# A hybrid decoder layer's expert phase: gates put into the one-hots by ScalarE, expert numbers found by row and column, the second product opened with the first tiles, and the second table's rows spread over all its tiles

## The chip, the core and the metric

The kernel runs on one core of one Trainium2 chip. The metric is device time in microseconds (us) of one execution. A kernel's time is the median of its runs. Times inside an execution come from one profiled execution, which has a time of its own.

## The reference, cut to what matters

The layer is a residual block: a mixer (RWKV-7 and dilated attention) gives `h`, and then 8 heads of a product-key expert layer add to it. Only the expert part is touched here. There are 512 tokens, 16384 experts, and 8 x 16 = 128 chosen experts for each token.

```python
def peer(u, peer_wq, peer_k1, peer_k2, peer_u, peer_v):
    ...
    v1, i1 = lax.top_k(s1, PEER_TOPK)                 # 16 of 128 row keys
    v2, i2 = lax.top_k(s2, PEER_TOPK)                 # 16 of 128 column keys
    cand = (v1[..., :, None] + v2[..., None, :]).reshape(cshape)
    cidx = (i1[..., :, None] * PEER_N_KEYS + i2[..., None, :]).reshape(cshape)
    top, sel = lax.top_k(cand, PEER_TOPK)             # 16 of 256 pairs
    idx = jnp.take_along_axis(cidx, sel, axis=-1)
    gate = jax.nn.softmax(top, axis=-1)
    ...
        ue = jnp.take(peer_u, ic, axis=0)
        act = jax.nn.gelu(jnp.einsum('cd,ced->ce', uc, ue).astype(jnp.float32), approximate=False)
        ve = jnp.take(peer_v, ic, axis=0)
        return jnp.einsum('ce,ced->cd', (gc * act).astype(ve.dtype), ve)
```

## The kernel before, in words

Tokens 0 to 127 are done as the reference does it, with gathered rows: GpSimd (POOL) gathers one expert row for every token of the group (128 gathers from `u`, 128 from `v`, 524 KB each, line 1146), and VectorE (DVE) takes the dot product (line 1155) or accumulates the row times its gate (line 1169). Six row buffers (`NUG`) are shared by both tables.

Tokens 128 to 511 (384 tokens) are done densely over all experts. **Product one** goes over 128 tiles of `uT`, each 128 experts: `gemm_ch` loads the tile (`wraw`, 512 KB, queue of SyncE, SP), splits it into a high part (`whi`, ScalarE (ACT), line 127) and a low part (`wlo`, DVE, line 128), and TensorE (PE) does 24 matmuls of 384 columns, three for each of 8 blocks. There are four buffers for the split tiles. ScalarE takes the result out of one of the two `mm` banks by a gelu (line 1208), and the tile goes to DRAM (`act_d`) unless it is one of NR = 8 tiles that stay in SBUF; these are the last 8.

Beside product one run two background programs. `rows_u` is the gathers from the first table. `routing` alternates `topk` and `scatter`. `topk` finds the 16 best pairs of each token among 50 candidates (`cand`), with the pair's expert number in `cidx` (POOL adds); it gets the number out by a one-hot of 16 x 50 (`eq`, lines 1081 to 1084) for each head. `scatter` spreads the gates into a dense matrix G[expert, token], four tokens a step, 96 steps: one one-hot of the column index for four tokens (`ohE`, DVE, line 1127), four one-hots of the row index that are multiplied by the gate in the same instruction (`ohA`, DVE, line 1131), four matmuls of 128 columns in fp32 (line 1137, eight records, in the four banks `c` to `f` by turns), and an ACT copy into `Gs` (line 1138). Every 8 steps ACT writes a 2 MB block to DRAM (`g_d`).

**Product two** goes over 128 tiles of `v`. A `G` block (8 tiles, 1.5 MB) and the gelu tile `act` are loaded by SP, DVE multiplies them (line 1249), ACT makes `wh` (line 1255) and DVE `wl` (line 1256), and 18 matmuls of 512 columns add the tile's part to six banks (`mm`, `mm`, `a`, `a`, `c`, `d`), which stay open over all 128 tiles. The order of the tiles begins with the eight kept ones (120 to 127). `G` holds gates of every token, so it needs the last `g_d` write. `rows_v` runs beside it.

The order of instructions on each engine comes from a scheduler with a simulated timeline (`schedule_with_timeline_sim`): ready work is put earlier than the code says, so the order on the engines is not that of the loops. Each engine, and each DMA queue with it, then works strictly in its order. Two conditions hold whatever the scheduler does: the pool `vg`, with `G`, `wh` and `wl`, takes the place of `pp`, the pool of `topk` and `scatter`, so none of its tiles exists before that pool is closed; and `vp`, with the residual `hfin`, takes the place of `n2`, which the last matmul of product one reads.

Of the kernel before, what the change touches and what calls it, by code (L numbers as in the profile page):

```python
# [100 lines left out]
class Kern:  # L101
# [947 lines left out]
    def topk(self, pp, i, res):  # L1049
# [5 lines left out]
        nc.vector.tensor_scalar(xf[:, :, 0], xf[:, :, 0], 128.0, None, op0=OP.mult)  # L1055
        cand = pp.tile([P, 8, NCAND], F32, tag="cand", name="cand")
        cidx = pp.tile([P, 8, NCAND], F32, tag="cidx", name="cidx")
# [20 lines left out]
        xs = pp.tile([P, 8, 16], F32, tag="xs", name="xs")  # L1078
        for h in range(8):
            eq = pp.tile([P, 16, NCAND], F32, tag="eq", name="eq", bufs=2)  # L1080
            nc.vector.tensor_tensor(eq, self.iota[:, None, :NCAND].to_broadcast([P, 16, NCAND]),
                                    posf[:, h, :, None].to_broadcast([P, 16, NCAND]), op=OP.is_equal)
            nc.vector.tensor_tensor(eq, eq, cidx[:, h, None, :].to_broadcast([P, 16, NCAND]), op=OP.mult)
            nc.vector.tensor_reduce(xs[:, h], eq, axis=AX.X, op=OP.add)
            if h % 2:
                yield
# [8 lines left out]
        if i == 0:  # L1095
            xi = self.gp.tile([P, 8, 16], I32, name="xi0")
            nc.vector.tensor_copy(xi, xs)
# [5 lines left out]
        xi = pp.tile([P, 8, 16], I32, tag="xi", name="xi")  # L1103
        x2 = pp.tile([P, 8, 16], I32, tag="x2", name="x2")
        nc.vector.tensor_copy(xi, xs)
        nc.vector.tensor_scalar(x2, xi, 127, None, op0=OP.bitwise_and)
        nc.vector.tensor_copy(sel[:, 1], x2)
        nc.vector.tensor_scalar(x2, xi, 7, None, op0=OP.logical_shift_right)
        nc.vector.tensor_copy(sel[:, 0], x2)
# [8 lines left out]
    def scatter(self, pp, i, res):  # L1118
# [67 lines left out]
    def phase_peer(self, es):  # L1186
# [7 lines left out]
        self.iota = pp.tile([P, 128], F32, name="iota")  # L1194
# [6 lines left out]
        done = 0  # L1201
        for i1 in range(128):
            acc = self.gemm_ch(I["uT"][i1], KT, n2h, n2l)
            if i1 < 128 - NR:
# [4 lines left out]
            if i1 < 128 - NR:  # L1209
# [12 lines left out]
        order = list(range(128 - NR, 128)) + list(range(128 - NR))  # L1222
# [4 lines left out]
        rows = self.rows_v(acc0)  # L1227
        LAST = 4
# [8 lines left out]
        for n, i1 in enumerate(order):  # L1237
            if n % GI == 0:
                G = vg.tile([P, TD // GB, GI, GB], F32, tag="G", name="G", bufs=2)
# [104 lines left out]
```

## Time and profile before

| | |
|---|---|
| median of 3 runs | 2067.61 us (2065.8 to 2068.58) |
| the profiled execution: its time | 2073.24 us |
| the profiled execution: its span | 2071.4 us |
| mean granted TensorE clock | 0.975 of full speed |
| PE busy | 1959.7 us, 95% of the span |
| DVE busy | 1606.0 us, 78% |
| ACT busy | 938.4 us, 45% |
| POOL busy | 639.8 us, 31% |
| DMA | 519.45 MB, mean 251 GB/s |
| PE work on the chain that ended last | 62%; DVE 17%, DMA 11% |

The span is the time between the first and the last instruction that the profiler saw; the execution's own time is 1.84 us longer. The experts take the stretch from about 870 us to the end. The shares are means over stages with different limits, so the rows further down are taken stage by stage.

### The profile page before, as it was taken

Reading aid. Unit: us, or ns where it says so; the run is one execution under the profiler, and the core shown is the slowest. Engines: PE = TensorE matmul, PEld = TensorE weight load, DVE = VectorE, ACT = ScalarE, POOL = GpSimd, SP = SyncE. Lnnn points to the kernel's source line nnn. Section 1 sums busy time; section 2 is a strip of 40 time slices with the busy share of each in tenths; the row PEclk is TensorE's granted clock in tenths of the full one; section 3 lists DMA queues with packets and bytes.
Section 4 is the critical chain, followed back from the end, with each engine's and each line's share of the span. In section 5 each row is a group of like instructions: output and inputs, shape, how many; then the busy total and the mean of one; then the engine's idle time right before and its main releaser. Section 6 shows DMA issues by size and latency. Waiting matters only on the chain.

```text
span 2071.4 us, 34017 instructions
## 1 busy us (share of the span) xinstructions
PE 1959.7 (95%) x12529; PEld 1699.5 (82%) x12529; DVE 1606.0 (78%) x3192; ACT 938.4 (45%) x1454; POOL 639.8 (31%) x511
## 2 busy tenths in 40 slices
PE   5998899999998979999999999999959999989999
PEld 4676677788877868899999999999948887778887
DVE  7476895955645548999999999877769988888555
ACT  3756666564354343343344544466623333334332
POOL 2324650331411110005755445400034555450000
PEclk9999989999999989999999999999979999999999
DMA  6666855356556313248988999965499999998763
GB/s 267 212 205 194 254 175 148 107 194 217 175 184 213 128 62 120 92 163 315 356 332 325 363 347 349 371 250 215 172 364 365 394 397 369 397 363 322 227 214 115
DMA packets 236299, 519.45 MB, mean 251 GB/s; under 512 B 35554, under 2 KB 129506, under 8 KB 233572
## 3 DMA queue, kind: packets, MB, share of 16 engines
q1 hardware_dynamic: 180260, 334.27, 47.1%
q0 software_dynamic: 36864, 134.23, 17.3%
q10 hardware_dynamic: 19008, 48.77, 6.2%
q8 instruction: 99, 1.62, 0.3%
q14 instruction: 68, 0.56, 0.1%
HBM read 432.23 MB, written 84.97 MB: 250 GB/s over the span
## 4 chain that ended last, share of the span: by engine, by line
PE 62%; DVE 17%; DMA 11%; issue 5%; ACT 3%; POOL 2%; SPq 0%; DVEq 0%; ACTq 0%; POOLq 0%
PE ps_mm L141 14%; PE ps_mm L143 13%; PE ps_mm L142 13%; DMA act<-act_d 4%; PE gps L1137 4%; DVE wlo L128 4%; DVE row L1155 2%; DMA wada<-in_wada 2%; PE ps_a L143 2%; PE ps_a L141 2%; PE ps_a L142 2%; DMA wraw<-in_v 2%; DVE acc L1169 1%; DMA G<-g_d 1%; POOL acc L443 1%
## 5 line engine op out<-in xcount | busy, mean ns | idle before, releaser
L127 ACT ACTIVATE whi<-wraw 128x1024 fp32r<-128x1024 f32 x356 | 370.1, 1042 | 399.7 <-PE ps_mm L142 223.6
L128 DVE TENSOR_TENSOR wlo<-wraw,whi 128x1024 fp32r<-128x1024 f32 x356 | 431.9, 1216 | 133.4 <-ACT whi L127 128.3
L141 PE MATMUL ps_mm<-n2h,whi 128*128 128x384 f32 (+1 forms) x1152 | 400.3, 348 | 3.2 <-ACT act L1208 3.2
L142 PE MATMUL ps_mm<-n2l,whi 128*128 128x384 f32 (+1 forms) x1152 | 398.4, 346 | 0.0
L143 PE MATMUL ps_mm<-n2h,wlo 128*128 128x384 f32 (+1 forms) x1152 | 396.2, 345 | 2.2 <-DVE wlo L128 2.2
L1146 POOL DMA_INDIRECT row<-in_v,xi x128 | 196.9, 1538 | 346.1 <-DVE acc L1169 173.1
L1146 POOL DMA_INDIRECT row<-in_u,xi x128 | 186.9, 1460 | 171.9 <-DVE dots L1155 133.6
L141 PEld LDWEIGHTS ps_mm<-n2h,whi 128*128 128x128 f32 x1152 | 218.5, 190 | 9.1 <-ACT act L1208 4.4
L143 PEld LDWEIGHTS ps_mm<-n2h,wlo 128*128 128x128 f32 x1152 | 218.3, 190 | 8.3 <-DVE wlo L128 3.4
L142 PEld LDWEIGHTS ps_mm<-n2l,whi 128*128 128x128 f32 x1152 | 218.5, 190 | 4.7
L141 PE MATMUL ps_mm<-n1h,whi 128*128 128x512 f32 x464 | 191.9, 417 | 6.5 <-ACT n1h L271 5.0
L1255 ACT ACTIVATE wh<-act 128x384 fp32r<-128x384 f32 x128 | 66.8, 526 | 280.1 <-DVE act L1249 148.9
L142 PE MATMUL ps_mm<-n1l,whi 128*128 128x512 f32 x464 | 190.3, 410 | 0.2 <-DVE n1l L272 0.2
L143 PE MATMUL ps_mm<-n1h,wlo 128*128 128x512 f32 x464 | 190.2, 410 | 0.0
L1169 DVE SCALAR_TENSOR_TENSOR acc<-row,g,acc 128x1024 f32<-128x1024 f32 x127 | 162.3, 1278 | 0.8
L1155 DVE CUSTOM_DVE_ANT_0 row<-row,n2t 128x1024 f32<-128x1024 f32 x128 | 153.0, 1217 | 0.5 <-DMA row<-in_u,xi 0.5
L1249 DVE TENSOR_TENSOR act<-act,G 128x384 f32<-128x384 f32 x128 | 69.9, 553 | 105.3 <-DMA act<-act_d 90.6
L1138 ACT ACTIVATE Gs<-gps 128x512 f32<-128x512 f32 x96 | 107.0, 1120 | 57.1 <-PE gps L1137 55.1
L141 PE MATMUL ps_mm<-whi,wh 128*128 128x512 f32 x256 | 93.1, 397 | 33.8 <-ACT wh L1255 33.8
L141 PEld LDWEIGHTS ps_mm<-n1h,whi 128*128 128x128 f32 x464 | 90.7, 197 | 29.3 <-ACT n1h L271 5.0
L142 PEld LDWEIGHTS ps_mm<-n1l,whi 128*128 128x128 f32 x464 | 90.6, 195 | 21.2 <-issue 2.5
L143 PEld LDWEIGHTS ps_mm<-n1h,wlo 128*128 128x128 f32 x464 | 91.0, 196 | 20.7 <-issue 0.8
(406 smaller groups left out, 3883.0 us busy)
## 6 DMA issues: line engine op xcount, KB each, us to landing
wraw<-in_uT SPq DMA_DIRECT2D x128, 512.0 KB, 5.5
wraw<-in_v SPq DMA_DIRECT2D x128, 512.0 KB, 7.9
wraw<-in_win SPq DMA_DIRECT2D x60, 512.0 KB, 4.0
g_d<-Gs ACTq DMA_DIRECT2D x12, 2048.0 KB, 10.3
G<-g_d SPq DMA_DIRECT2D x16, 1536.0 KB, 11.9
act_d<-act ACTq DMA_DIRECT2D x120, 192.0 KB, 5.2
act<-act_d SPq DMA_DIRECT2D x120, 192.0 KB, 8.2
wada<-in_wada SPq DMA_DIRECT2D x64, 256.0 KB, 4.2
```

What stands on the lines that cost most here:

```text
L127: nc.scalar.activation(hi[:, :n], raw[:, :n], AF.Copy)
L128: nc.vector.tensor_tensor(lo[:, :n], raw[:, :n], hi[:, :n].bitcast(F32), op=OP.subtract)
L141: mm(acc, lh, rh, start=start, stop=False)
L142: mm(acc, lh, rl, start=False, stop=False)
L143: mm(acc, ll, rh, start=False, stop=stop)
L1137: nc.tensor.matmul(g[:, j], E[:, j], A[:, j], start=True, stop=True)
L1138: nc.scalar.activation(Gs[:, :, o:o + 4].rearrange("p i t -> p t i"), g, AF.Copy)
L1146: self.nc.gpsimd.indirect_dma_start(row, None, self.I[tab], bass.IndirectOffsetOnAxis(ap=self.xi[:, n:n + 1], axis=0))
L1155: self.gathered(self.rowp, n, "u", lambda row: nc.vector.tensor_tensor_reduce(out=row, in0=row, in1=self.n2t, scale=1.0, scalar=0.0, op0=O ...
L1169: nc.vector.scalar_tensor_tensor(acc, row, self.gates0[:, n:n + 1], acc, op0=OP.mult, op1=OP.add)
L1249: nc.vector.tensor_tensor(act.rearrange("p (b t) -> p b t", t=GB), act.rearrange("p (b t) -> p b t", t=GB), G[:, :, n % GI, :], op=OP.mult)
L1255: nc.scalar.activation(wh, act, AF.Copy)
```

## The change

In `topk`, the expert number is no longer read out of `cidx`, which is gone with its POOL adds. Row and column are found apart: `ge` says which candidate rows begin at or before the position, its product with the steps `dx` between neighbouring row keys sums up to the row, and its product with the lengths of the rows gives the position inside the row, whose one-hot picks the column. Two heads go in one instruction, so there are 16 groups of 8 instructions of 512 elements in place of 32 groups of 3 instructions of 800 elements. The second and third sums go straight into `sel`, so the casts and shifts that took a number apart are gone. The constant `iota` grows from 128 to 160 columns.

In `scatter`, one DVE instruction makes both one-hots for four tokens (`ohAE`, 1024 elements, three buffers), and ACT multiplies the four row one-hots by the gates (128 columns each, the gate as a per-partition scale).

In `phase_peer`, the kept tiles are 0 to 7, product two goes over its tiles in order 0 to 127, the background has to be done by tile 112 in place of 119, the pool `pp` is closed there and the first `G` block is asked for. Three tiles are weighed (`act` times `G`, `wh`, `wl`) while product one still runs, and the banks are filled in the order `a`, `c`/`d`, `mm`. In the code `rows_v` takes n x 128 // 118 steps by tile n in place of one for each tile and a second one at every sixteenth from 80 on.

```diff
@@ topk
-        nc.vector.tensor_scalar(xf[:, :, 0], xf[:, :, 0], 128.0, None, op0=OP.mult)
+        dx = pp.tile([P, 8, 16], F32, tag="dx", name="dx")
+        nc.vector.tensor_copy(dx[:, :, 0:1], xf[:, :, 0, 0:1])
+        nc.vector.tensor_tensor(dx[:, :, 1:], xf[:, :, 0, 1:], xf[:, :, 0, :15], op=OP.subtract)
...
-            nc.gpsimd.tensor_tensor(cidx[:, :, o:o + n], xf[:, :, 0, p:p + 1].to_broadcast([P, 8, n]),
-                                    xf[:, :, 1, 0:n], op=OP.add)
...
-        for h in range(8):
-            eq = pp.tile([P, 16, NCAND], F32, tag="eq", name="eq", bufs=2)
-            nc.vector.tensor_tensor(eq, self.iota[:, None, :NCAND].to_broadcast([P, 16, NCAND]),
-                                    posf[:, h, :, None].to_broadcast([P, 16, NCAND]), op=OP.is_equal)
-            nc.vector.tensor_tensor(eq, eq, cidx[:, h, None, :].to_broadcast([P, 16, NCAND]), op=OP.mult)
-            nc.vector.tensor_reduce(xs[:, h], eq, axis=AX.X, op=OP.add)
...
+        for h0 in range(0, 8, 2):
...
+            nc.vector.tensor_tensor(ge, ph[:, :, None].to_broadcast([P, n, 16]), row(128), op=OP.is_ge)
+            nc.vector.tensor_tensor(by_head(eq), by_head(ge), dx[:, hs, None, :].to_broadcast([P, 2, 16, 16]), op=OP.mult)
+            nc.vector.tensor_reduce(sel[:, 0, hs].rearrange("p h k -> p (h k)"), eq, axis=AX.X, op=OP.add)
+            nc.vector.tensor_tensor(ge, ge, row(144), op=OP.mult)
+            off = pp.tile([P, n], F32, tag="off", name="off", bufs=2)
+            nc.vector.tensor_reduce(off, ge, axis=AX.X, op=OP.add)
+            nc.vector.tensor_tensor(off, ph, off, op=OP.subtract)
+            nc.vector.tensor_tensor(eq, off[:, :, None].to_broadcast([P, n, 16]), row(0), op=OP.is_equal)
+            nc.vector.tensor_tensor(by_head(eq), by_head(eq), xf[:, hs, 1, None, :].to_broadcast([P, 2, 16, 16]), op=OP.mult)
+            nc.vector.tensor_reduce(sel[:, 1, hs].rearrange("p h k -> p (h k)"), eq, axis=AX.X, op=OP.add)
@@ scatter
-            nc.vector.tensor_tensor(E, self.iota[:, None, :].to_broadcast([P, 4, 128]),
-                                    sl[:, 1, t4:t4 + 4, None].to_broadcast([P, 4, 128]), op=OP.is_equal)
+            AE = pp.tile([P, 2, 4, 128], F32, tag="ohAE", name="ohAE", bufs=3)
+            A, E = AE[:, 0], AE[:, 1]
+            nc.vector.tensor_tensor(AE, self.iota[:, None, None, :128].to_broadcast([P, 2, 4, 128]),
+                                    sl[:, 0:2, t4:t4 + 4, None].to_broadcast([P, 2, 4, 128]), op=OP.is_equal)
             for j in range(4):
                 t = t4 + j
-                nc.vector.tensor_scalar(A[:, j], self.iota, sl[:, 0, t:t + 1], sl[:, 2, t:t + 1],
-                                        op0=OP.is_equal, op1=OP.mult)
+                nc.scalar.activation(A[:, j], A[:, j], AF.Copy, scale=sl[:, 2, t:t + 1])
@@ phase_peer
+        def weigh(i1, act):
+            nc.vector.tensor_tensor(act.rearrange("p (b t) -> p b t", t=GB), act.rearrange("p (b t) -> p b t", t=GB),
+                                    Gs[i1 - i1 % GI][:, :, i1 % GI, :], op=OP.mult)
...
+            nc.scalar.activation(wh, act, AF.Copy)
+            nc.vector.tensor_tensor(wl, act, wh.bitcast(F32), op=OP.subtract)
...
-            if i1 < 128 - NR:
+            if i1 >= NR:
                 act = ap.tile([P, TD], F32, tag="act", name="act", bufs=4)
...
-            while done < min(i1 + 1, 10) + max(i1 - 9, 0) * 96 // 104:
+            while done < min(i1 + 1, 10) + max(i1 - 9, 0) * 96 // 98:
...
-            if i1 == 119:
+            if i1 == 112:
                 run(bg)
                 e1.close()
                 vg = self.pool(es, "vg")
+                load_g(0)
+            elif i1 >= 120 and i1 % 2 == 0 and len(ready) < 3:
+                weigh(len(ready), keep[len(ready)])
...
-        order = list(range(128 - NR, 128)) + list(range(128 - NR))
...
-                for t in out:
+                for t in (2, 3, 1):
...
-            next(rows, None)
-            if n > 64:
-                next(rows, None) if n % 16 == 0 else None
+            while vdone < n * 128 // 118:
+                next(rows_v, None)
+                vdone += 1
```

How the instructions of SyncE's queue stand around the end of product one. Before (`wraw<-in_uT` and `wraw<-in_v` are the weight tiles of product one and two; the first row comes after ten earlier `uT` loads):

```order
L124 DMA wraw<-in_uT 128x1024 x117
L1248 DMA act<-act_d 128x384 x3
L124 DMA wraw<-in_uT 128x1024
L1248 DMA act<-act_d 128x384
L124 DMA wraw<-in_v 128x1024 x8
L1240 DMA G<-g_d 128x12x256 x2
L1242 DMA hfin<-h_d 128x4x1024
L1243 DMA gt_15109<-gt_d 128x1024
L1240 DMA G<-g_d 128x12x256
L124 DMA wraw<-in_v 128x1024 x5
```

And now, on the same queue and again after ten earlier loads:

```order
L124 DMA wraw<-in_uT 128x1024 x107
L1212 DMA G<-g_d 128x12x256 x2
L124 DMA wraw<-in_uT 128x1024 x2
L1212 DMA G<-g_d 128x12x256
L124 DMA wraw<-in_uT 128x1024 x9
L124 DMA wraw<-in_v 128x1024 x7
L1267 DMA hfin<-h_d 128x4x1024
L1273 DMA act<-act_d 128x384 x3
L1268 DMA gt_15011<-gt_d 128x1024
L124 DMA wraw<-in_v 128x1024 x2
```

The two `G` loads were behind the first eight tiles of `v`; they now stand eleven tiles of `uT` before the end of product one. The residual `hfin` and the first `act` loads stand between the tiles of `v`.

How ScalarE's instructions stand in the scatter stretch, late in product one. Before (`whi` is the high part of the next weight tile, `act` the gelu, `Gs` the copy of a scatter step):

```order
L127 ACTIVATE whi<-wraw 128x1024
L1208 ACTIVATE act<-ps_mm 128x384
L1210 DMA act_d<-act 128x384
L1138 ACTIVATE Gs<-gps 128x4x128 x2
L127 ACTIVATE whi<-wraw 128x1024
L1208 ACTIVATE act<-ps_mm 128x384
```

And now (`ohAE` is the gate's multiplication into the row one-hots, four for each step):

```order
L1137 ACTIVATE ohAE<-ohAE,sl 128x128 x8
L1232 ACTIVATE act<-ps_mm 128x384
L1143 ACTIVATE Gs<-gps 128x4x128
L1234 DMA act_d<-act 128x384
L1137 ACTIVATE ohAE<-ohAE,sl 128x128 x4
L1143 ACTIVATE Gs<-gps 128x4x128 x2
L1137 ACTIVATE ohAE<-ohAE,sl 128x128 x4
L1145 DMA g_d<-Gs 128x4096
L1137 ACTIVATE ohAE<-ohAE,sl 128x128 x4
L127 ACTIVATE whi<-wraw 128x1024
```

Every scatter step now has two visits on ScalarE, one ahead of its matmuls and one behind them. On DVE the 96 pairs of one-hots stand between the `wlo` of `uT` tile 39 and that of tile 108; before, they stood between that of tile 47 and that of `v` tile 3.

How DVE's instructions stand in product two, while rows of the second table come in. Before (`acc` takes one gathered row):

```order
L1169 SCALAR_TENSOR_TENSOR acc_15110<-row,g_8687,acc_15110 128x1024
L1249 TENSOR_TENSOR act<-act,G 128x384
L1169 SCALAR_TENSOR_TENSOR acc_15110<-row,g_8687,acc_15110 128x1024
L1256 TENSOR_TENSOR wl<-act,wh 128x384
L1249 TENSOR_TENSOR act<-act,G 128x384
L128 TENSOR_TENSOR wlo<-wraw,whi 128x1024
L1256 TENSOR_TENSOR wl<-act,wh 128x384
L1169 SCALAR_TENSOR_TENSOR acc_15110<-row,g_8687,acc_15110 128x1024 x2
L1249 TENSOR_TENSOR act<-act,G 128x384
L128 TENSOR_TENSOR wlo<-wraw,whi 128x1024
```

And now:

```order
L1174 SCALAR_TENSOR_TENSOR acc_15012<-row,g_8689,acc_15012 128x1024
L1216 TENSOR_TENSOR act<-act,G 128x384
L1174 SCALAR_TENSOR_TENSOR acc_15012<-row,g_8689,acc_15012 128x1024
L1223 TENSOR_TENSOR wl<-act,wh 128x384
L1174 SCALAR_TENSOR_TENSOR acc_15012<-row,g_8689,acc_15012 128x1024 x2
L1216 TENSOR_TENSOR act<-act,G 128x384
L128 TENSOR_TENSOR wlo<-wraw,whi 128x1024
L1223 TENSOR_TENSOR wl<-act,wh 128x384
L1216 TENSOR_TENSOR act<-act,G 128x384
L128 TENSOR_TENSOR wlo<-wraw,whi 128x1024
L1223 TENSOR_TENSOR wl<-act,wh 128x384
```

The rows are grouped otherwise, but in both orders 12 stand to every 8 tiles, and the last row stands behind the `wlo` of `v` tile 85 before and of tile 86 now.

## Rows read from the trace of the kernel before

**Rows 1.** One line's instructions: gelu of product one (ns min/median/max, first and last start us).

```profile
L1208 ACT ACTIVATE act<-ps_mm x128: 466/472/553, 873.1 to 1497.5; 128x384 f32<-128x384 f32 x128
```

**Rows 2.** Timeline of ACT: gelus nine tiles apart, and two neighbours in the scatter stretch.

```profile
1001.69 0.49 ACT L1208 ACTIVATE act<-ps_mm 128x384 f32<-128x384 f32 x1 [3.67 <-PE ps_mm L143]
...
1039.13 0.49 ACT L1208 ACTIVATE act<-ps_mm 128x384 f32<-128x384 f32 x1 [1.20 <-PE ps_mm L143]
...
1402.13 0.47 ACT L1208 ACTIVATE act<-ps_mm 128x384 f32<-128x384 f32 x1
...
1408.09 0.47 ACT L1208 ACTIVATE act<-ps_mm 128x384 f32<-128x384 f32 x1
```

**Rows 3.** Windows in product one: us, PE, PEld, DVE, ACT, POOL busy (count), PEclk, DMA share, GB/s.

```profile
1048.00:1112.00 64.00, 59.05 (x332) 57.23 (x331) 64.00 (x135) 26.91 (x34) 29.43 (x22) 0.92 0.84 305
1360.00:1480.00 120.00, 120.00 (x809) 120.00 (x808) 91.34 (x226) 74.28 (x83) 0.00 (x0) 1.00 0.57 209
```

**Rows 4.** Timeline from product one to product two: start, us, engine, line [idle before <-releaser].

```profile
1501.44 1.17 PE L1137 MATMUL gps<-ohA,ohE 128*128 128x128 f32 x8 [1.60 <-DVE ohA L1131]
...
1503.74 0.33 ACTq L1140 DMA_DIRECT2D g_d<-Gs  x1
...
1511.23 4.29 SPq L1240 DMA_DIRECT2D G<-g_d  x2
...
1523.13 3.84 DVE L1249 TENSOR_TENSOR act<-act,G 128x384 f32<-128x384 f32 x8 [14.45 <-DMA G<-g_d]
...
1524.30 0.79 PE L141 MATMUL ps_mm<-whi,wh 128*128 128x512 f32 x1 [21.69 <-ACT wh L1255]
```

**Rows 5.** Windows there: the wait itself, and two microseconds behind it (columns as before).

```profile
1503.70:1524.30 20.60, 0.00 (x0) 0.00 (x0) 6.04 (x7) 0.59 (x3) 5.82 (x5) 0.52 1.00 355
...
1526.00:1528.00 2.00, 2.00 (x6) 1.52 (x6) 2.00 (x4) 0.00 (x0) 0.00 (x0) 0.50 1.01 398
```

**Rows 6.** Timeline of PE: two tiles of product two, and the last matmul.

```profile
2030.10 0.39 PE L141 MATMUL ps_mm<-whi,wh 128*128 128x512 f32 x1
...
2034.18 0.39 PE L141 MATMUL ps_mm<-whi,wh 128*128 128x512 f32 x1
...
2065.91 0.39 PE L143 MATMUL ps_d<-whi,wl 128*128 128x512 f32 x1
```

**Rows 7.** Windows in product two: two with rows of `v` coming in, one after the last.

```profile
1524.30:1684.00 159.70, 159.70 (x696) 132.08 (x697) 146.42 (x171) 56.82 (x77) 85.31 (x55) 0.99 1.02 383
1684.00:1884.00 200.00, 188.27 (x812) 152.52 (x811) 172.42 (x199) 67.12 (x89) 97.38 (x63) 0.99 1.02 379
1924.00:2044.00 120.00, 120.00 (x531) 99.36 (x530) 67.05 (x94) 45.01 (x62) 0.00 (x0) 1.00 0.64 208
```

**Rows 8.** PE's waits from 1530 to the end: us in total, times, longest.

```profile
PE ps_mm L141 <- ACT wh L1255: 12.1, 9, 3.4
```

**Rows 9.** DMA from 1530 to 1880.

```profile
DMA packets 54262, 133.15 MB, mean 380 GB/s; under 512 B 4457, under 2 KB 29142, under 8 KB 54239
```

**Rows 10.** DVE's groups by form, 865 to 1510: xcount | busy us, mean ns | idle before.

```profile
L1131 DVE TENSOR_SCALAR ohA<-iota,sl 128x128 f32<-128x128 f32 x384 | 106.6, 342 | 0.0
L1127 DVE TENSOR_TENSOR ohE<-iota,sl 128x512 f32<-128x512 f32 x96 | 65.6, 683 | 8.9 <-PE gps L1137 8.8
L1081 DVE TENSOR_TENSOR eq<-iota,posf 128x800 f32<-128x800 f32 x32 | 30.9, 979 | 0.0
```

**Rows 11.** ACT's groups by form, whole span or from 865 to 1510.

```profile
L127 ACT ACTIVATE whi<-wraw 128x1024 fp32r<-128x1024 f32 x129 | 136.3, 1063 | 181.4 <-PE ps_mm L142 137.7 <-DMA wraw<-in_uT 22.9 <-issue 4.3
L1138 ACT ACTIVATE Gs<-gps 128x512 f32<-128x512 f32 x96 | 107.0, 1120 | 57.1 <-PE gps L1137 55.1
L441 ACT ACTIVATE wada<-wada,silc 128x512 f32<-128x512 f32 x56 | 39.5, 717 | 37.3 <-DMA wada<-in_wada 37.1
L884 ACT ACTIVATE sc<-sc,ot 128x128 f32<-128x128 f32 x32 | 12.4, 390 | 11.8 <-DVE ot L882 10.5 <-issue 1.3
```

**Rows 12.** Timeline of ACT: three instructions with a per-partition scale, back to back.

```profile
267.07 1.93 ACT L441 ACTIVATE wada<-wada,silc 128x512 f32<-128x512 f32 x3
```

More of the change, by code (lines that the diff above doesn't have):

```diff
@@ L1102, in topk @@
             return
[L1103 to L1109, printed above, removed]
         tp = self.ps("a")
@@ L1193, in phase_peer @@
         pp = self.pool(e1, "pp")
-        self.iota = pp.tile([P, 128], F32, name="iota")
+        self.iota = pp.tile([P, 160], F32, name="iota")
         nc.sync.dma_start(self.iota, I["iota"])
@@ L1201, in phase_peer, with load_g @@
         done = 0
+        ready, Gs = {}, {}
+        LAST = 4
+        def load_g(i1):
+            G = Gs[i1] = vg.tile([P, TD // GB, GI, GB], F32, tag="G", name="G", bufs=2)
+            nc.sync.dma_start(G, self.g_d[:, :, i1:i1 + GI, :].rearrange("b p i t -> p b i t"))
+        def weigh(i1, act):
+            nc.vector.tensor_tensor(act.rearrange("p (b t) -> p b t", t=GB), act.rearrange("p (b t) -> p b t", t=GB),
+                                    Gs[i1 - i1 % GI][:, :, i1 % GI, :], op=OP.mult)
+            tail = i1 >= 128 - LAST
+            bufs, tg, pool = (LAST, "f", vp) if tail else (3, "", vg)
+            wh = pool.tile([P, TD], F32R, tag="wh" + tg, name="wh", bufs=bufs)
+            wl = pool.tile([P, TD], F32R, tag="wl" + tg, name="wl", bufs=bufs)
+            nc.scalar.activation(wh, act, AF.Copy)
+            nc.vector.tensor_tensor(wl, act, wh.bitcast(F32), op=OP.subtract)
+            ready[i1] = wh, wl
         for i1 in range(128):
             acc = self.gemm_ch(I["uT"][i1], KT, n2h, n2l)
-            if i1 < 128 - NR:
+            if i1 >= NR:
                 act = ap.tile([P, TD], F32, tag="act", name="act", bufs=4)
@@ L1226, in phase_peer @@
         acc0 = vp.tile([P, D], F32, name="acc0")
-        rows = self.rows_v(acc0)
-        LAST = 4
+        rows_v = self.rows_v(acc0)
+        vdone = 0
         def mms(t, f, ws, n):
@@ L1236, in phase_peer @@
         last = []
-        for n, i1 in enumerate(order):
-            if n % GI == 0:
-                G = vg.tile([P, TD // GB, GI, GB], F32, tag="G", name="G", bufs=2)
-                nc.sync.dma_start(G, self.g_d[:, :, i1:i1 + GI, :].rearrange("b p i t -> p b i t"))
+        for n in range(128):
+            if n % GI == 0 and n not in Gs:
+                load_g(n)
             if n == 64:
@@ L1243, in phase_peer @@
                 nc.sync.dma_start(gt2, self.gt2_d)
-            if i1 in keep:
-                act = keep[i1]
-            else:
-                act = ap.tile([P, TD], F32, tag="act", name="act", bufs=4)
-                nc.sync.dma_start(act, self.act_d[i1])
-            nc.vector.tensor_tensor(act.rearrange("p (b t) -> p b t", t=GB), act.rearrange("p (b t) -> p b t", t=GB),
-                                    G[:, :, n % GI, :], op=OP.mult)
-            bufs = LAST if n >= 128 - LAST else 3
-            tg = "f" if n >= 128 - LAST else ""
-            wh = (vp if tg else vg).tile([P, TD], F32R, tag="wh" + tg, name="wh", bufs=bufs)
-            wl = (vp if tg else vg).tile([P, TD], F32R, tag="wl" + tg, name="wl", bufs=bufs)
-            nc.scalar.activation(wh, act, AF.Copy)
-            nc.vector.tensor_tensor(wl, act, wh.bitcast(F32), op=OP.subtract)
-            hi, lo = self.wtile(I["v"][i1 * 128:(i1 + 1) * 128, :])
-            ws = (wh, wl, hi, lo)
+            if n not in ready:
+                act = keep.get(n)
+                if act is None:
+                    act = ap.tile([P, TD], F32, tag="act", name="act", bufs=4)
+                    nc.sync.dma_start(act, self.act_d[n])
+                weigh(n, act)
+            hi, lo = self.wtile(I["v"][n * 128:(n + 1) * 128, :])
+            ws = (*ready[n], hi, lo)
             if n < 128 - LAST:
-                for t in out:
+                for t in (2, 3, 1):
                     for f in range(2):
@@ L1264, in phase_peer @@
                 last.append((n, ws))
-            next(rows, None)
-            if n > 64:
-                next(rows, None) if n % 16 == 0 else None
-        run(rows)
+            while vdone < n * 128 // 118:
+                next(rows_v, None)
+                vdone += 1
+        run(rows_v)
         for t in range(NT):
@@ L1325, in host @@
     a["v"] = f(w["peer_v"])
-    a["iota"] = np.tile(np.arange(128, dtype=np.float32), (128, 1))
+    o = np.array([o for o, _ in CAND])
+    a["iota"] = np.tile(np.concatenate([np.arange(128), o, np.diff(o, prepend=0)]).astype(np.float32), (128, 1))
     a["masks"] = f(np.concatenate(mask, axis=1))
```

20 lines of the change are left out of this document (12 added, 8 removed).

## The prediction

> **What bounds the kernel now.** I read the experts' part in three stages, each by the view that shows its limit. First product one, by one line's starts: the 128 gelus begin from 873.1 to 1497.5 us [rows 1], 624.4 us. Nine tiles without scatter take 1001.69 to 1039.13, so 4.16 us a tile; a tile with two scatter steps takes 5.96, so a step costs PE 0.90 [rows 2]. 127 x 4.16 + 92 x 0.90 = 611.1 (four of the 96 steps stand behind the last gelu), so some 13 us are lost; an estimate of 1 is for topk's transposes. The windows show where: from 1048 to 1112 DVE is busy without a gap, PE for 59.05 of 64 us at a granted clock of 0.92, while from 1360 to 1480 PE is full at 1.00 with DVE at 91 and ACT at 74 of 120 [rows 3]. So DVE bounds a short stretch and PE the rest.
>
> Second the transition, by the timeline: the last scatter matmul ends at 1502.6 and the first matmul of product two starts at 1524.30 after 21.69 us of waiting for `wh`, which waits for DVE's `act` times G, which waits for G; the last `g_d` issue is at 1503.74, SP gets to the G loads at 1511.23 [rows 4]. DMA is full in these 20.6 us at 355 GB/s, and the granted clock is 0.52, still 0.50 (the level of 1.2 GHz) between 1526 and 1528 [rows 5].
>
> Third product two: a tile is 4.08 us at full clock, the last matmul ends at 2066.30 [rows 6], so 542.0 us for 128 x 4.08 = 522.2: 19.8 are lost. The windows say to what: while rows of `v` come in, the DMA engines are full at 383 and 379 GB/s and PE sinks to 188 of 200 us; after the last row DMA is at 0.64 and PE full [rows 7]. PE's waits there are 12.1 us, all on `wh` [rows 8], behind late `act` tiles. A tile needs 0.524 MB of `v`, 0.197 of `act`, 0.197 of G and 1.5 rows of 0.524: 1.70 MB, at 4.08 us 417 GB/s against the 380 delivered [rows 9]. Product two is DMA-bound until the rows end, at 4.48 us a tile, and PE lives on a head start.
>
> **The change part by part.**
>
> *First tiles open product two.* The G loads stand eleven tiles before the end of product one, and `wh` of three tiles is made there, so the wait goes with what it brings: 1.60 + 21.69 us [rows 4], and the half clock behind it, at most 4.3 us of work at half speed, an estimate of 2.1 [rows 5]. Together -25.4.
>
> *What takes its place there.* G still needs the last `g_d` write. The last scatter step now stands between tiles 107 and 108, T0. Issue of `g_d` 1.6 after that, some 7 to land (2 MB at 355 GB/s is 5.9), two G blocks of 1.57 MB some 12 more (8.9 at that rate, beside other loads): G is there at about T0 + 21. The order asks ACT for `wh` behind the gelu of tile 111, at T0 + 17, and what stands behind it on ACT, `whi` of the next weight tile, feeds PE. Split weights ahead of PE cover one to two tiles, 4 to 8 us. Between 0 and 5 us; I take +2.
>
> *DMA's head start.* In before's wait the queues moved 7.3 MB [rows 5] with PE idle. Of that five rows (2.62 MB) and `hfin` (2.10), with `gt2` (0.52), four `act` (0.79) and one `v` tile that were issued before, now fall into the DMA-bound stretch; one G block (1.57) leaves it. Net 5.0 MB, at 380 GB/s [rows 9] 13.1 us, less 4.1 because PE is one tile further when the rows end: 9. PE pays this only as far as its head start is used up, and it already loses there [rows 8]. Bounds 0 and 13; I take +8.
>
> *Rows over all tiles.* The loop asks for 1.08 rows a tile, but the order on DVE has 12 in 8 tiles as before, and the last one only a tile later. They are gathered as fast as buffers come free, so nothing is spread: 0. If it were, 1.08 rows would be 1.48 MB a tile, 364 GB/s: within the 380, and the 12.1 us and most of the 19.8 would go. That is a rival.
>
> *One-hots.* DVE loses 65.6 + 106.6 us [rows 10] and gains 96 instructions of 1024 elements, for which there is no row: 512 elements take 0.683 and 800 take 0.979 [rows 10], 1.03 ns for each more, which gives 1.21 for 1024, and twice 512 would be 1.37. That is 116 to 131, so -41 to -56. topk's three lines of 30.9 us [rows 10] become 128 of 512 elements at 0.683 or so, 87 plus some short ones: -5 to 0. The DVE-bound stretch of 64 us lost 4.95 by PE's idle time and some 5 by the clock, 0.08 of 64 [rows 3]. In the new order scatter starts 8 tiles earlier and row dots are pulled forward by 6 tiles, so the load is packed denser; adding up DVE's durations tile by tile against PE's, DVE falls behind by 3 us where it fell behind by 6. So half of this comes back at best, and -2 is what I take for product one; bounds -8 and the ACT case below.
>
> *ACT.* 384 multiplications of 128 columns. With a scale by partition and this width a row has 390 ns [rows 11]; three of 512 columns take 1.93 us where each has 717 [rows 11, 12], so in a row they are 0.11 closer. Four cost 3 x 0.28 + 0.39 = 1.23 us. A step then costs ACT 1.23 + 1.12 for `Gs` [rows 11] = 2.35. Between tiles 60 and 108 stand 69 steps: 69 x 2.35 = 162, and 48 tiles of `whi` 1.06 [rows 11], gelu 0.48 [rows 2] and an issue of 0.33 [rows 4] = 90. Sum 252 of PE's 48 x 4.16 + 69 x 0.90 = 262. ACT is filled to 96%, and at 0.39 without overlap to 105%. Full does not yet mean late: four banks for `gps`, three `ohAE` and four weight buffers stand between. I take 0 for the middle; at 105% it is +13.
>
> The Trainium skill, page "ScalarE: Activation LUTs", section "What ACT_TABLE_LOAD costs", speaks against this part: it gives an ACTIVATE 186 ns + 0.833 ns for each column and some 93 ns more for each pointer operand, so by an estimate 386 ns for 128 columns with a pointer scale, more than the 342 ns of the DVE instruction that it replaces, 148 us in all for ACT. The trace agrees: 390 here, and by the page 706 for 512 columns against 717 [rows 11]. The page says the overlap of neighbours is 93 ns, which would make the sum 255 in place of 252.
>
> *POOL's* candidate adds go; POOL is idle for most of that time and nobody waits for it: 0.
>
> **Sum.** -25.4 + 2 + 8 - 2 = -17.4, against the profiled execution's 2073.24 us: 2055.8. That execution is 5.6 above the median of the runs (2067.61), so for the median I say **2050.2**.
>
> **Rivals.**
>
> A (my forecast, own range 2043 to 2057), 0.46.
>
> B: the head start costs nothing, since the rows wait for DVE and buffers anyway, and DVE's relief gives 4 to 8 in product one. -25.4 - 4 = -29.4: 2038. For it: PE's waits in product two come in few pieces, 9 of at most 3.4 us [rows 8]. Against: DMA at 1.02 throughout [rows 7]. 0.15.
>
> C: the rows really spread and product two loses next to nothing: -25.4 + 2 - 2 - 17 = -42: 2025. Against it is the order on DVE. 0.04.
>
> D: ACT is the bound in the scatter stretch at 105%: +13 in place of 0: 2063. For it: two visits for each step, and ACT's order has up to eight multiplications in one piece ahead of a gelu, for 2.5 us in which a bank is not given back. Against: its 74 of 120 us before [rows 3]. 0.20.
>
> E, the other side: each step's chain runs DVE, ACT, PE, ACT, and ACT works strictly in order; if its multiplication waits for DVE's one-hot and the gelu behind it for that, PE loses at each of 96 steps. At 0.3 us a step, 29 us: 2079. It decides from 17.4 + 4 = 21.4 us, 0.22 a step. For it: DVE was full from 1048 to 1112, where scatter is now pulled to [rows 3]. Against: three buffers let the one-hot be made two steps ahead. 0.08.
>
> F: G is later than T0 + 21 and ACT waits before `whi`: PE stops for some 15 us in tiles 111 to 116 in place of 2: 2063. For it: in before, G took from 1511.23 to 1523.13 with nothing but rows and `hfin` beside it, and now `uT` runs. 0.07.
>
> **How the numbers follow.** What a measurement of this kernel can tell from no change is 0.2%, 4.1 us: faster is below 2063.5. A, B and C lie there whole, of D and F about half: 0.65 + 0.14 = 0.79. Same: the other half of D and F with A's upper tail cut off, 0.12. Slower: E, 0.09 with D at its worst. The range runs from B's 2038, less 2, to 2066, so that C, E and the far ends of D and F are outside, some 0.2.
>
> **What the profile after would show.** Transition: PE's longest wait between the last `uT` and first `v` matmul under 5 us, clock 1.0 there; if G is late, ACT waiting for `act` before 1480. Product one: first to last gelu within 620 to 630 us (it now holds all 96 steps, 614.7 by the prices above); if longer, PE waiting for `whi` or the gelu, with ACT at 95% or more in the windows, is D, and ACT idle on DVE's `ohAE` is E. `ohAE` on ACT near 390 ns and on DVE near 1210. Product two: DMA full for about as many tiles as before and PE's waits on `wh` some 20 us in place of 12.1; rows ending near tile 84. What would make me wrong most: the head start, whose +8 comes from bytes and not from a wait that a row shows.

## The result, and the profile after

The change takes the median from 2068.1 us (2065.8 to 2068.9, 4 runs) to 2046.6 us (2043.27 to 2050.33, 4 runs): ratio 0.9887, 95% interval 0.9871 to 0.9903. Forecast were 2050.2 and faster. The profiled execution took 2050.33 us with a span of 2048.5, 22.9 below that of before.

The first view is one line's starts, product one's gelus (count, ns min/median/max, first and last start):

```profile
L1232 ACT ACTIVATE act<-ps_mm x128: 465/490/622, 880.8 to 1510.8; 128x384 f32<-128x384 f32 x128
```

It starts 7.7 us later than before [rows 1]. No instruction of the mixer ahead of it is changed or moved, and over the profiles of this study this start lies anywhere between 871.6 and 880.8; so from here on the **experts' stretch** is compared, from the first gelu to the end of the span: 1198.3 us before, 1167.7 after, and 1167.2 in a second profile of the same instructions. Its gain, 30.6 us, is the spans' 22.9 and these 7.7, and larger than that of the medians, 21.5. One profile of each kernel stands behind it, and before's has a spell at a lower granted clock, 0.92 from 1048 to 1112 [rows 3], some 5 us of lost time, which after has not.

The second view is the timeline from product one to product two (PE's first and last matmuls, SP's G load, DVE's weighing):

```profile
1435.60 1.54 SPq L1212 DMA_DIRECT2D G<-g_d  x2
...
1444.85 3.84 DVE L1216 TENSOR_TENSOR act<-act,G 128x384 f32<-128x384 f32 x8 [5.40 <-DMA G<-g_d]
...
1500.59 0.63 PE L141 MATMUL ps_a<-whi,wh 128*128 128x512 f32 x2
...
1509.67 0.33 PE L143 MATMUL ps_mm<-n2h,wlo 128*128 128x384 f32 x1
1509.84 0.39 PE L142 MATMUL ps_a<-wlo,wh 128*128 128x512 f32 x1
...
2043.08 0.39 PE L143 MATMUL ps_d<-whi,wl 128*128 128x512 f32 x1
```

Where [rows 4] had 21.69 us of waiting, PE goes from the last matmul of product one (ending at 1510.00) to product two without a gap; four matmuls of product two's first tile even stand ahead of that end. G is asked for 75.6 us earlier. Third, the windows, with the columns of [rows 3]:

```profile
1048.00:1112.00 64.00, 61.34 (x384) 60.31 (x382) 64.00 (x119) 48.11 (x95) 29.78 (x21) 1.00 0.93 334
1488.00:1508.00 20.00, 20.00 (x116) 19.83 (x115) 6.11 (x6) 7.19 (x10) 0.00 (x0) 1.00 0.49 164
1508.00:1530.00 22.00, 22.00 (x101) 18.53 (x100) 16.92 (x19) 6.28 (x9) 10.29 (x7) 1.00 0.99 380
1530.00:1700.00 170.00, 169.01 (x743) 138.90 (x743) 155.56 (x179) 61.91 (x81) 87.76 (x60) 1.00 1.03 392
1700.00:1880.00 180.00, 173.76 (x750) 139.31 (x749) 165.77 (x194) 65.41 (x87) 78.29 (x55) 1.00 1.03 385
```

The granted clock stays at 1.00 through the transition [rows 5]. PE is still short of time while rows come in [rows 7]. Its waits, in product one and in product two:

```profile
PE ps_mm L141 <- ACT act L1232: 3.5, 4, 1.5
PE gps L1142 <- ACT ohAE L1137: 3.2, 5, 1.0
PE ps_mm L143 <- DVE wlo L128: 0.6, 2, 0.4
...
PE ps_a L141 <- ACT wh L1222: 7.2, 13, 1.7
```

The stretch adds up stage by stage. Product one with all scatter steps: 873.1 to 1502.6 before, 880.8 to 1510.0 after, less 0.9 for the four early matmuls of product two: -1.2. The wait: -21.7. Product two from its restart: 542.0 before, 2043.47 - 1510.0 + 0.9 = 534.4 after: -7.6, of which the half clock behind the wait is 2.1. Together -30.5 of 30.6. (The 2.1 is half of the 4.1 us from 1524.3 in which before's granted clock was still 0.50.)

Product one gives almost nothing, though DVE was relieved in it. PE's waits there are 7.3 us, 5.4 in before. And one stretch is held up by ACT, which those waits hardly list. From the gelu of tile 98 to that of tile 106 ACT is busy without a pause:

```profile
1364.10:1421.50 57.40, 56.55 (x378) 55.04 (x377) 35.68 (x31) 57.40 (x130) 0.00 (x0) 1.00 0.63 227
```

Eight tiles and some 22 scatter steps stand there (177 records of their matmuls, eight to a step). By the prices of [rows 2] they take 8 x 4.16 + 22 x 0.90 = 53.1 us of PE, so an estimated 4 us is lost to ACT.

### The profile page after: what moved, and what is told of

Same layout as the page of the kernel before. It is cut to its first block, busy times and chain, and to the rows that moved or that the text cites. A ratio compares the mean times of both kernels' runs of the same rounds, so it can differ in the third digit from the quotient of the medians.

```text
span 2048.5 us, 33924 instructions
## 1 busy us (share of the span) xinstructions
PE 1962.5 (96%) x12529; PEld 1698.7 (83%) x12529; DVE 1547.6 (76%) x2847; ACT 1036.3 (51%) x1838; POOL 601.5 (29%) x447
## 4 chain that ended last, share of the span: by engine, by line
PE 72%; DMA 10%; DVE 7%; ACT 7%; issue 3%; POOL 1%; SPq 0%; ACTq 0%; DVEq 0%; POOLq 0%
PE ps_mm L141 16%; PE ps_mm L143 16%; PE ps_mm L142 16%; DMA act<-act_d 3%; PE gps L1142 3%; PE ps_a L141 2%; PE ps_a L142 2%; PE ps_a L143 2%; DMA wada<-in_wada 2%; DMA G<-g_d 1%; DMA wraw<-in_v 1%; DVE acc L1174 1%; ACT ohAE L1137 1%; DVE wlo L128 1%; ACT Gs L1143 1%
## 5 line engine op out<-in xcount | busy, mean ns | idle before, releaser
L1151 POOL DMA_INDIRECT row<-in_v,xi x128 | 184.9, 1445 | 332.7 <-DVE acc L1174 161.1
L1133 DVE TENSOR_TENSOR ohAE<-iota,sl 128x1024 f32<-128x1024 f32 x96 | 116.1, 1221 | 14.2 <-PE gps L1142 14.1
L1137 ACT ACTIVATE ohAE<-ohAE,sl 128x128 f32<-128x128 f32 x384 | 122.2, 409 | 5.4 <-ACT act L1232 3.4
L1142 PE MATMUL gps<-ohAE 128*128 128x128 f32 x768 | 110.6, 278 | 3.3 <-ACT ohAE L1137 3.2
```

Of the source, the lines that this page charges most:

```text
L1133: nc.vector.tensor_tensor(AE, self.iota[:, None, None, :128].to_broadcast([P, 2, 4, 128]), sl[:, 0:2, t4:t4 + 4, None].to_broadcast([P, 2, ...
L1137: nc.scalar.activation(A[:, j], A[:, j], AF.Copy, scale=sl[:, 2, t:t + 1])
L1142: nc.tensor.matmul(g[:, j], E[:, j], A[:, j], start=True, stop=True)
L1151: self.nc.gpsimd.indirect_dma_start(row, None, self.I[tab], bass.IndirectOffsetOnAxis(ap=self.xi[:, n:n + 1], axis=0))
```

## The experiments

Two theories stood against each other. **P** is the prediction's: the wait between the products goes because the first tiles are kept and weighed early, and DVE's relief is worth 2 us. **Q**: the wait was long because scatter, paced by DVE, ended only with product one. Three kernels took the change apart.

**One-hots and topk alone** (the kernel before with the new `topk` and `scatter`):

```diff
+            AE = pp.tile([P, 2, 4, 128], F32, tag="ohAE", name="ohAE", bufs=3)
...
+                nc.scalar.activation(A[:, j], A[:, j], AF.Copy, scale=sl[:, 2, t:t + 1])
```

> The kernel before with the new topk and the new one-hots (DVE's pair, ScalarE's multiplication), everything else as before: kept tiles are the last eight, G is asked for where the scheduler puts it, rows rule as before. Theory P (the prediction's steps: the transition's 25.4 us go because the first tiles are kept and weighed early; DVE's relief is worth 2): 2063 to 2068 us. Theory Q (the transition was long because scatter, paced by DVE, ended with product one; once DVE is relieved, scatter ends early and the old tile order loses its wait as well): 2043 to 2052 us, last scatter matmul near tile 113, PE's longest wait between the products under 6 us.

Measured: 2051.39 us, ratio 0.9904 (0.9885 to 0.9923), experts' stretch 1169.7, no PE wait between the products. The last scatter matmul ends at 1437.0, 59 us ahead of product one's end, and the scheduler by itself now puts both G loads there, with the old tile order:

```profile
1447.84 1.63 SPq L1245 DMA_DIRECT2D G<-g_d  x2
```

**First tiles alone** (the changed kernel with `topk`, one-hots and rows rule of before):

```diff
-            AE = pp.tile([P, 2, 4, 128], F32, tag="ohAE", name="ohAE", bufs=3)
+            E = pp.tile([P, 4, 128], F32, tag="ohE", name="ohE", bufs=2)
+            A = pp.tile([P, 4, 128], F32, tag="ohA", name="ohA", bufs=2)
```

> The changed kernel with topk, the one-hots and the rows rule of before, so the new tile order, the early weighing and the bank order alone. Theory P: 2043 to 2053 us. Theory Q: scatter still ends behind product one, so G comes as late as before and PE waits 15 to 25 us between the products: 2062 to 2071 us.

Measured: 2071.09 us against 2071.87 of before on that chip, ratio 0.9996 (0.9979 to 1.0012). PE's waits there are as in [rows 4]:

```profile
PE ps_a L141 <- ACT wh L1217: 21.5, 1, 21.5
PE gps L1137 <- DVE ohA L1131: 1.8, 2, 1.6
```

In its one profile the experts' stretch is 1193.1, 5 us under before's, nearly all of it in product two (536.2 from its restart); the medians show no gain. The wait (with the columns of [rows 3]), and its first and last matmul of product two:

```profile
1508.10:1529.65 21.55, 0.02 (x1) 0.00 (x0) 7.06 (x8) 1.65 (x3) 5.85 (x5) 0.53 0.97 348
```

```profile
1529.65 0.79 PE L141 MATMUL ps_a<-whi,wh 128*128 128x512 f32 x1 [21.54 <-ACT wh L1217]
...
2065.49 0.39 PE L143 MATMUL ps_d<-whi,wl 128*128 128x512 f32 x1
```

**The change without the one-hots** (both made by DVE; new `topk`, tile order and rows rule stay):

```diff
-                nc.scalar.activation(A[:, j], A[:, j], AF.Copy, scale=sl[:, 2, t:t + 1])
+                nc.vector.tensor_scalar(A[:, j], self.iota[:, :128], sl[:, 0, t:t + 1], sl[:, 2, t:t + 1],
+                                        op0=OP.is_equal, op1=OP.mult)
```

> The changed kernel with both one-hots made by DVE as before (new topk, new tile order, new rows rule stay). Theory P: within 4 us of the changed kernel, 2043 to 2051 us. Theory Q: the scheduler puts the last one-hots at tile 126, G is late again: 2058 to 2070 us, with a wait of 12 to 24 us between the products.

Measured: 2067.64 us, ratio 0.9979 (0.9963 to 0.9994), experts' stretch 1192.1. The last scatter matmul ends at 1491.2, where the changed kernel's ends at 1424.8, and G came late as Q says. But the price showed elsewhere than expected: one wait of 5.4 us at the transition, and then PE short of work in product two from 1610 on. Its waits there are for split weights (8.5 us for `whi`, 7.7 for `wlo`); that product two began without a head start is a likely reason, which no run tests:

```profile
1610.00:1730.00 120.00, 114.04 (x495) 92.00 (x494) 102.55 (x121) 39.68 (x53) 69.09 (x40) 1.00 1.03 394
1730.00:1880.00 150.00, 140.51 (x595) 112.43 (x594) 127.84 (x148) 49.18 (x65) 82.81 (x49) 0.98 1.00 370
```

P falls: most of the gain belongs to the one-hots with the new `topk` (0.0096 of the change's 0.0113), and without the one-hots everything else together gives 0.0021. The new tile order, which looks like the cause, gives the medians nothing without them. With them it is worth 2 us of the experts' stretch (1169.7 against 1167.7, one profile each), and the intervals of the two ratios overlap. The new `topk` alone was not run.

**The old rows rule in the changed kernel**:

```diff
-            while vdone < n * 128 // 118:
-                next(rows_v, None)
-                vdone += 1
+            next(rows_v, None)
+            if n > 64:
+                next(rows_v, None) if n % 16 == 0 else None
```

> The changed kernel with the rows rule of before. The order of instructions is that of the changed kernel on every engine, so if only the order counts: 2043 to 2050 us, and product two loses the same 12 us or so as in the changed kernel. Rival C's root (the rule itself spreads the rows): some 5 to 10 us slower than the changed kernel, 2052 to 2057 us.

Measured: 2046.17 us, ratio 0.9885 (0.9863 to 0.9907), experts' stretch 1167.2. The rule changes nothing; these are the changed kernel's instructions.

The next question was what still costs product two some 12 us. **Without 122 of the 128 rows of the second table**:

```diff
-            self.gathered(self.rowp, n, "v", use)
+            if n < 6:
+                self.gathered(self.rowp, n, "v", use)
```

> The changed kernel without the gathers and sums of 122 of the 128 rows of the second table (left out: these rows' part of the output for tokens 0 to 127). Theory H (product two's loss of some 12 us is DMA's: too many bytes a tile while rows come in): the loss falls under 2 us, 2033 to 2038 us. Rival K (the loss is late issue of act tiles on SP or short waits of ACT and DVE, whatever the load): 6 us or more of it stays, 2041 to 2047 us.

Measured: 2046.47 us, ratio 0.9882 (0.986 to 0.9903). A miss for H: in the window below DMA ran at two thirds, and PE still waited 6.9 us in product two, at `wl`, in 8 pieces. The window and the timeline of the longest:

```profile
1707.00:1747.00 40.00, 37.41 (x158) 30.31 (x157) 19.85 (x29) 13.40 (x18) 0.00 (x0) 0.96 0.66 208
...
1730.57 0.56 DVE L1217 TENSOR_TENSOR act<-act,G 128x384 f32<-128x384 f32 x1 [7.28 <-DMA act<-act_d]
1731.65 0.79 PE L143 MATMUL ps_a<-whi,wl 128*128 128x512 f32 x1 [2.60 <-DVE wl L1224]
```

Here the scheduler, with DVE free, asked for each `act` tile only as it was needed, and one that stood behind a G load came late. Another order gives another loss, so this run doesn't measure what DMA costs in the changed kernel.

**Residual and gate after the last row, in the row buffers**; and, in a second kernel, with the accumulator off the memory of `n2` as well:

```diff
-        h = vp.tile([P, NT, D], F32, name="hfin")
-        gt2 = vp.tile([P, D], F32, name="gt2")
...
+        late = [self.rowp.tile([P, D], F32, tag="row", name="row", bufs=NUG) for _ in range(5)]
+        for t in range(NT):
+            nc.sync.dma_start(late[t], self.h_d[t])
```

> The changed kernel with the residual and the gate (2.62 MB) loaded into the row buffers after the last row, so out of the DMA-bound stretch; rows begin where they did. If PE pays for bytes as the prediction's head start term has it: 2.62 MB at 390 GB/s, 5 to 7 us faster than the changed kernel, 2038 to 2043 us. If rows and act tiles wait for buffers and DVE rather than for bytes: no difference, 2044 to 2049 us.

> As the last one, and the accumulator lies outside the memory of n2, so rows of the second table begin in product one (first at tile 112, last at v tile 69 in place of 86), where DMA has room. Theory H: nearly all of the 12 us come back, 2033 to 2039 us. Rival K: 2042 to 2049 us.

Measured: 2074.86 us, ratio 1.0016 (0.9998 to 1.0034), for the first, and 2047.47, 0.9897 (0.9874 to 0.9921), for the second. Both miss. In the first, ACT sat idle for up to 12.9 us until a weight tile came, and in the window below PE is idle for 6 of 40 us at a granted clock of 0.91, with DMA at 0.94:

```profile
ACT whi L127 <- DMA wraw<-in_v: 63.5, 15, 12.9
...
1628.00:1668.00 40.00, 33.67 (x137) 27.04 (x136) 32.11 (x38) 12.13 (x16) 19.03 (x13) 0.91 0.94 347
```

SP's loads of `v` and of `act` now partly stand in pairs, where they alternated. It decides nothing about bytes, but shows that the same loads in another order can cost 28 us, what the lower clock takes among them. In the second, rows begin and end 17 tiles earlier, and product two still loses some 11 us, in a shorter stretch: PE is busy 194.35 of 200 us from 1584 to 1784, at 396 GB/s. Beginning the rows earlier does not help where they stand as dense as before.

**Rows really spread**: three buffers for the second table's rows, in place of six:

```diff
-            self.gathered(self.rowp, n, "v", use)
+            self.gathered(self.vrow, n, "v", use, "rv", 3)
```

> The changed kernel with three row buffers of their own for the second table, so that the order on DVE has 7 to 10 rows to each 8 tiles up to the last tile in place of 12 up to tile 86; the residual is loaded into the old row buffers during product one. 1.0 rows a tile is 1.45 MB, 355 GB/s at 4.08 us. Theory H and rival C's price: the loss goes nearly whole, 2033 to 2039 us. Against it: three buffers leave only 12 us for a gather, and if a row lands later, DVE and then PE wait in order: 2045 to 2060 us.

Measured: 2039.16 us, ratio 0.9853 (0.9833 to 0.9873), experts' stretch 1162.0 against the changed kernel's 1167.7 and 1167.2. On DVE 7 to 10 rows stand to 8 tiles, with 13 in the last 8. PE has no wait in product two at all:

```profile
1547.00:1987.00 440.00, 440.00 (x1942) 364.45 (x1942) 358.68 (x428) 159.34 (x216) 129.32 (x102) 1.00 0.97 347
```

It gives 3 us back at the end (last rows and sums behind the last matmul) and 3.9 in product one (2.63 and 1.26), where G, asked for beside more loads, is late, and ACT waits for it with the gelu behind (timeline):

```profile
1442.40 3.84 DVE L1216 TENSOR_TENSOR act<-act,G 128x384 f32<-128x384 f32 x8 [9.51 <-DMA G<-g_d]
...
1443.00 0.52 ACT L1222 ACTIVATE wh<-act 128x384 fp32r<-128x384 f32 x1 [6.82 <-DVE act L1216]
...
1445.83 0.45 PE L141 MATMUL ps_mm<-n2h,whi 128*128 128x384 f32 x1 [2.63 <-ACT act L1232]
```

That is rival F's mechanism, which the changed kernel mostly escapes: there the same wait of ACT is 2.7 us, and PE loses 0.8, at 1454.7, behind a weight tile that was loaded after G.

So the number of row buffers sets how dense the scheduler puts the rows: six give 12 to 8 tiles, three of their own 7 to 10, and five, as the next run shows, 10. **Five row buffers, nothing else**:

```diff
-NUG = 6
+NUG = 5
```

> The changed kernel with five row buffers in place of six (NUG = 5), one number. The order on DVE then has 10 rows to each 8 tiles up to tile 101 in place of 12 up to tile 86: 1.25 rows, 1.57 MB a tile, 386 GB/s at 4.08 us, about what the queues gave in the changed kernel. Theory R (the number of row buffers sets how densely rows come, and that density, over what DMA delivers, makes product two's loss): the loss falls from 12 us to 0 to 5, 2036 to 2043 us, experts' stretch 1156 to 1163 us. Rival (five buffers hold up the first table's rows in product one): product one gets 4 us or more longer and takes the gain back, 2044 to 2052 us.

Measured: 2023.31 us (2019.01 to 2026.69, 5 runs), ratio 0.9776 (0.9758 to 0.9794): twice the gain of the change, and better than either theory said. Gelus, and windows in both products:

```profile
L1232 ACT ACTIVATE act<-ps_mm x128: 465/473/570, 872.5 to 1491.6; 128x384 f32<-128x384 f32 x128
```

```profile
1048.00:1112.00 64.00, 64.00 (x410) 64.00 (x410) 64.00 (x129) 48.10 (x94) 31.91 (x20) 1.00 0.91 326
1535.00:1695.00 160.00, 160.00 (x708) 132.48 (x707) 144.12 (x169) 61.87 (x80) 64.71 (x50) 1.00 1.04 392
1695.00:1875.00 180.00, 180.00 (x796) 149.05 (x795) 161.89 (x188) 68.97 (x89) 65.25 (x55) 1.00 1.03 385
```

Product two waits for nothing, with the DMA engines as full as ever and nearly the same GB/s. Product one is 10.9 us shorter (619.1 against 630.0), of which PE's waits explain 5 (2.0 in place of 7.3 in the changed kernel). Some 4 more lie where ACT held PE up in the changed kernel: the same eight tiles (98 to 106) take 52.4 us in place of 57.4 with some 21 steps in place of 22, by the prices 52.2. So the order of the scatter steps moved too, with this one number. The experts' stretch is 1144.7. Fewer gathers on the way at one time and rows that stand less dense go together here; no run tells them apart.

**Three G buffers**:

```diff
-            G = Gs[i1] = vg.tile([P, TD // GB, GI, GB], F32, tag="G", name="G", bufs=2)
+            G = Gs[i1] = vg.tile([P, TD // GB, GI, GB], F32, tag="G", name="G", bufs=3)
```

> The changed kernel with three buffers for G in place of two. PE's waits in product two stand within 1 us of a G issue in the changed kernel, because SP holds its queue there until the buffer of two blocks before is free. Theory K (SP's hold at G makes the next act and weight loads late): those waits go, product two loses under 6 us, 2037 to 2042 us. Theory R (bytes): the DMA load is the same, the loss stays at 10 to 12 us, 2043 to 2050 us.

Measured: 2041.88 us, ratio 0.9873 (0.9849 to 0.9896), experts' stretch 1166.4 against 1167.2 and 1167.7. Its time lies in K's range, but the waits do not go, and the time is within the scatter of the changed kernel's; K falls:

```profile
PE ps_a L141 <- ACT wh L1222: 6.3, 14, 1.2
```

**Gates multiplied twice**, for ACT's room:

```diff
                 nc.scalar.activation(A[:, j], A[:, j], AF.Copy, scale=sl[:, 2, t:t + 1])
+                nc.scalar.activation(A[:, j], A[:, j], AF.Copy)
```

> The changed kernel with a second ACT instruction of 128 columns behind each gate multiplication (384 more, a copy onto itself, no other result). The scheduler then ends scatter at tile 119 and asks for G at 126. If ACT has the room that its 77% in the scatter stretch says: product one within 5 us of the changed kernel, and 8 to 16 us of waiting for G at the transition, 2053 to 2065 us. If ACT is near its limit (rivals D and E): ACT's sum is 462 us for PE's 419 from tile 39 to 119, product one 35 to 50 us longer, 2080 to 2100 us.

Measured: 2051.27 us, ratio 0.9908 (0.9886 to 0.9931), experts' stretch 1172.7, 5 us more. From 1112 to 1360, the changed kernel and this one:

```profile
1112.00:1360.00 248.00, 248.00 (x1588) 247.50 (x1588) 232.74 (x330) 189.04 (x376) 105.25 (x73) 1.00 0.96 351
```

```profile
1112.00:1360.00 248.00, 246.57 (x1564) 245.53 (x1563) 225.98 (x319) 220.42 (x573) 102.97 (x72) 1.00 0.94 345
```

ACT takes 31 us more there and PE loses 1.4. Product one is 6.5 us longer, a little over the 5 expected; the G wait of 8 to 16 us didn't come: G was asked for at 1482.6 and lay hidden.

**Five row buffers in the kernel before**:

```diff
-NUG = 6
+NUG = 5
```

> The kernel before with five row buffers in place of six, nothing else. Theory R: product two loses 0 to 5 us in place of 17.7 behind its restart, product one some 5 to 10 less, and the transition's wait of 21 to 25 us stays, since scatter still ends with product one: 2040 to 2050 us, experts' stretch 1170 to 1182 us. If five buffers help only where DVE has been relieved: 2058 to 2068 us.

Measured: 2057.55 us against 2073.93 on that chip, ratio 0.9921 (0.9898 to 0.9945); the stretch, 1179.8, is as expected, the time 7.6 us over its range and just under the rival's, with before itself 5.8 higher on that chip than in the first result. Product two from its restart takes 525.4 in place of 542.0, so 3.2 us over 128 x 4.08, all but nothing beyond the half clock behind the wait. So five buffers help product two without any relief of DVE. Product one takes 619.6 in place of 624.4, and the wait stays:

```profile
PE ps_mm L141 <- ACT wh L1255: 20.7, 1, 20.7
```

## Why the prediction was right, and where it was not

The time was near, in part by luck: the cause behind the largest term was wrong, and the term for the head start had the wrong sign. By stages this pair of profiles gives 30.5 us where 17.4 were forecast, and the mixer, which the change doesn't touch, ended 7.7 us later in the profile after.

- *First tiles open product two, -25.4.* The size was right: 21.7 + 1.6 of waits and the half clock behind them went. The cause was wrong. The step credited the tile order and gave the one-hots -2; alone the tile order gives 0.9996 and the one-hots 0.9904. DVE's 172 us of one-hots [rows 10] became 116.1, and only with that does scatter end near tile 108, so that G is there (1424.8 us; 1491.2 with DVE's one-hots and the rest of the change). The order rows ahead of the prediction showed both edits at work at once; the order of each edit alone would have told them apart.
- *What takes its place, +2.* 0.8 measured; the 3.9 us of the three-buffer kernel show the mechanism, inside the bounds of 0 and 5.
- *DMA's head start, +8.* This step failed: product two lost less than before (12.2 in place of 19.8, the half clock's 2.1 among them), and PE's waits on `wh` fell to 7.2 us where some 20 were forecast. The kernel with the first tiles alone has the changed kernel's tile order and still the wait, 21.5 us in which DMA moves 348 GB/s with PE idle. Its product two loses 536.2 - 522.2 = 14.0, of which the half clock behind the wait is an estimated 1.8. That leaves 12.2, and the changed kernel, without the wait, loses 12.2 too: there the head start is worth nothing. (The kernel with DVE's one-hots, whose wait is 5.4, loses 551.0 - 522.2 = 28.8, so a late start can cost much; no run separates why.) Rival B said that the head start costs nothing, but its 4 to 8 us in product one did not come. The step took the 380 GB/s of [rows 9] for what the queues can give; after, they give 392 and 385. And it priced moved bytes, where the density of rows goes with the loss: the kernel whose rows began 17 tiles earlier lost 11 us, and with five buffers nothing is lost at 385 to 392 GB/s. The kernels with the old tile order lose more (before 17.7 without the half clock, the one-hots alone 18.7, the lower clock of 0.98 from 1700 to 1880 among it). So the tile order seems to give some 3 to 6 us there; one profile of each is all there is.
- *Rows over all tiles, 0.* Right, and for the reason given: the order is the same with either rule. Its rival C had about the right price for a true spreading (-17 for product two; the five-buffer kernel and the three-buffer kernel lose nothing there), but not the lever: the rows follow the buffers, not the loop.
- *One-hots and ACT.* DVE's pair takes 1221 ns (1.21 forecast), ACT's multiplication 409 (390 forecast), four of them 1.27 us by the busy time (122.2 for 384). ACT's fill was put too high as a mean, 82% busy from tile 60 to tile 108 (1161 to 1430) against 96%, but it is not even: 76% from 1112 to 1360 and 100% from 1364 to 1421, which costs an estimated 4 us where the sum had 0. So D's mechanism is real at its small end; its +13 is refuted, since doubled multiplications cost product one 6.5 us. E's chain shows in 3.2 us of PE's waits on `ohAE`, in 5 pieces, where E had 29. Product one gave -1.2 for -2, or +0.4 without the 1.60 us that the sum had counted in the wait's term.
- *The time.* The five-buffer kernel's stretch of 1144.7 us stands against 128 x 4.16 + 96 x 0.90 + 128 x 4.08 = 1141.1, by the prices of [rows 2, 6]: PE is nearly full there, and before's 57 us above it were the 23 of the wait, 18 to 20 in product two and the rest, in the main, in product one.

By an estimate from the Trainium skill, "ScalarE: Activation LUTs", section "What ACT_TABLE_LOAD costs" (186 ns, 0.833 ns for each column and some 93 ns for a pointer operand), the new multiplication takes 386 ns; the median here is 393. That rule spoke against this part by the engine's own cost, and it is right on the cost: what it says nothing of is that the engine that gave the work away was the one that paced scatter.

## What to carry to other kernels

When several edits go together, look at the instruction order of each alone before crediting one: the edit that asks for data early is worth little if another engine still makes that data late. Moving work to an engine that takes longer for it pays when the engine it leaves sets the pace of what the next stage waits for. A ring's size sets how tightly a scheduler packs background work, and a smaller ring can be the faster one: one buffer fewer gave about as much again as the whole change (0.9776 against 0.9887).

## What the runs showed that was not expected

- One row buffer fewer takes the stretch from 1167 to 1145 us. Of its half in product one (10.9 us), 5 are in the waits that the profile lists and some 4 where ACT was busy without a pause; about 2 are open.
- PE without any wait at 385 to 392 GB/s and DMA 1.03 to 1.04 busy, and with 2.8 to 3.5% of PE's time lost at 385 to 396 and the same share: the DMA engines' busy share doesn't tell whether a load is late.
- The same mixer instructions end 9 us apart in different profiles.
